# FFN up projections by seven block products instead of eight, with a separate down phase and a new grid for the operand pools

## The chip, the cores and the metric

The kernel runs on one core of a Trainium2 chip. The metric is the device time of one execution in microseconds (us), as the median of several runs; less is better. Engines: TensorE (PE; PEld is its weight load), VectorE (DVE), ScalarE (ACT), GpSimd (POOL), and SyncE (SP), which issues most DMA transfers.

## What is computed

Two layers of a decoder trunk on 1024 tokens of width 1024, all in float32. Layer 0 mixes with latent attention (MLA), layer 1 with a gated spatial unit (gMLP). What the change touches is the FFN that follows each mixer; after it a gated embedding (PLE) is added:

```python
for i in range(2):
    h = h + mixer_i(rms_norm(h, norm_mix[i]))          # mla_mixer / gmlp_mixer, ends in @ w_out
    hn = rms_norm(h, norm_ffn[i])                      # 1024 x 1024
    h = h + square(relu(hn @ ffn_w_up[i])) @ ffn_w_down[i]    # 1024 -> 4096 -> 1024
    hn = rms_norm(h, norm_ple[i])
    h = h + sigmoid(hn @ ple_w_gate[i]) * (p[i] @ ple_w_proj[i])
```

## The kernel before

The residual stream `h` stands in SBUF with features on the partitions: eight tiles `h0` to `h7` of 128 features x 1024 tokens. A float32 product is made of three TensorE products of operands split into a high and a low half (`split`: ScalarE casts the high half, VectorE subtracts it for the low one): high x high, high x low, low x high. A matmul has a 128x128 block of weights as its stationary operand and 512 tokens as its moving one.

`load_block` fetches 128x4 rows x 256 columns of weights (512 KB) by DMA into `raw` (pool `pr`, 3 buffers) and splits it into `wh` and `wl` (pool `pw`). `gemm` issues the matmuls of one block of 128 output rows into PSUM. `Norm.add` prepares the next phase's input as soon as a tile of `h` is final: `add_split` scales it by the gain and splits it into pool `phn`, `add_square` adds its square to `acc`. The factor 1/rms is applied only after the product: `sums` adds up `acc` over the partitions with four matmuls, `roots` takes the inverse root on ScalarE and VectorE.

`ffn` goes through the 4096 hidden features in eight slices of 512. For each slice it makes the up products (4 row blocks x 2 halves of the tokens x 8 blocks of depth x 3 = 192 matmuls), applies ReLU, the norm factor and the square, splits the result into `ah` and `al` (pool `pa`), and at once makes the slice's part of the down product (`down_slice`, another 192 matmuls) and adds it to `h`; the last slice goes through `down_sweeps`, which also prepares the next norm. Ahead of the FFN stands the mixer's output projection, a `down_slice` too: `wo1` in layer 0, `go3` in layer 1, in four blocks of 256 output rows. Behind each two tiles of `h` that it finishes, `nxt.add` prepares the FFN's input.

Nothing but the order of the program and the buffers of the pools sets the order on an engine: each engine takes its instructions in the order in which a scheduler has put them, and a pool hands its buffers out in program order.

SBUF addresses: the operand pools `pa`, `pw`, `pr`, `ph`, `pt` begin at 800 modulo 2048 bytes, `pb` at 832 behind its small `lead` tile, `phn` at 864.

Of the kernel before, what the change touches and what calls it, by code (L numbers as in the profile page):

```python
# [16 lines left out]
P = 128  # L17
T = 1024
# [14 lines left out]
QB, PB = 2, 2  # L33
LNEXP = "natural_log_exp_and_others"
# [5 lines left out]
def trunk(ctx: ExitStack, tc: tile.TileContext, I, out):  # L40
# [6 lines left out]
    pw = ctx.enter_context(tc.tile_pool(name="pw", bufs=6))  # L47
# [32 lines left out]
    G.memset(pb.tile([P, 8], F32, tag="lead", name="lead"), 0.0)  # L80
# [89 lines left out]
    class Norm:  # L170
# [72 lines left out]
        def tokens(self, c, pp=None):  # L243

            if self.r is None:
                self.r = pb.tile([P, NB], F32, tag="rtok", name=f"{self.name}_r")
# [4 lines left out]
            V.tensor_copy(self.r[:, c * 4:c * 4 + 4], pp.rearrange("p (b q) -> p b q", q=P)[:, :, 0])  # L251


    halves = {}

    def ffn(i, h, nrm, nxt, late):
        up, down = I["ffn_w_up"][i], I["ffn_w_down"][i]
        for s in range(FF // 512):
            ah = pa.tile([P, 4, T], F32R, tag="a", name=f"f{i}_ah{s}")
            al = pa.tile([P, 4, T], F32R, tag="a", name=f"f{i}_al{s}")  # L260
            for g in range(2):
                f0 = s * 512 + g * 256
                bl = [load_block(up, k0, f0) for k0 in (0, 4)]
                for f in range(2):
                    units = gemm(bl, nrm.hn, f, f"f{i}u{s}{g}{f}")
                    if nrm.rb is None:
                        for c in range(2):
                            nrm.sums(c, pso(f"f{i}st{c}"))
                        nrm.roots(0, 1)
                    rb = nrm.rb  # L270
                    t = tmp(f"f{i}t{s}{g}{f}")
                    k = 2 * g + f
                    for u, c in units:
                        V.scalar_tensor_tensor(t[:, c], u, 0.0, rb[:, c], op0=ALU.max, op1=ALU.mult)  # L274
                        S.activation(t[:, c], t[:, c], AF.Square)  # L275
                        S.copy(ah[:, k, c], t[:, c])
                        V.tensor_tensor(al[:, k, c], t[:, c], f32(ah[:, k, c]), op=ALU.subtract)
            rhs = chunked(ah, al, 4)
            if s == 1:
                halves[i] = p_split(i)  # L280
            if s < FF // 512 - 1:
                down_slice(down, 4 * s, rhs, h, f"f{i}d{s}", None)
            else:
                down_sweeps(down, 4 * s, rhs, h, f"f{i}d{s}", nxt, late)

    def down_slice(w, k0, rhs, h, name, nxt, seq=False):
        for q in range(4):
            bl = [load_block(w, k0, q * 256)]
            for f in range(2):
                j = 2 * q + f  # L290
# [96 lines left out]
    def gmlp(h, nrm, nxt):  # L387
# [85 lines left out]
        for gp in range(4):  # L473
# [58 lines left out]
            down_slice(w_out, 4 * gp, chunked(yh, yl, 4), h, f"go{gp}", nxt if gp == 3 else None, seq=True)  # L532
# [584 lines left out]
    n1 = Norm("n1", gain(1, 0))  # L1117
# [50 lines left out]
```

## Time and profile before

| | |
|---|---|
| median of 3 runs | 2728.8 us (2728.18 to 2729.13) |
| profiled execution, its own time | 2726.77 us |
| its span | 2725.0 us |
| granted TensorE clock, mean | 0.999 |
| TensorE busy, matmuls | 2691.1 us, 13600 |
| VectorE, ScalarE, GpSimd busy | 1228.5, 903.2, 317.0 us |
| DMA | 163.54 MB, mean 60 GB/s |

The profile shows one execution. Busy times are sums over all stages; what a stage waits for is read in the chain of waits, which follows the work that ended last back through the span, and in the timeline. Line numbers L.. are those of the kernel.

### The profile page before, as it was taken

Reading aid. Unit: us, or ns where it says so; the run is one execution under the profiler, and the core shown is the slowest. Engines: PE = TensorE matmul, PEld = TensorE weight load, DVE = VectorE, ACT = ScalarE, POOL = GpSimd, SP = SyncE. Lnnn points to the kernel's source line nnn. Section 1 sums busy time; section 2 is a strip of 40 time slices with the busy share of each in tenths; the row PEclk is TensorE's granted clock in tenths of the full one; section 3 lists DMA queues with packets and bytes.
Section 4 is the critical chain, followed back from the end, with each engine's and each line's share of the span. In section 5 each row is a group of like instructions: output and inputs, shape, how many; then the busy total and the mean of one; then the engine's idle time right before and its main releaser. Section 6 shows DMA issues by size and latency. Waiting matters only on the chain.

```text
span 2725.0 us, 33466 instructions
## 1 busy us (share of the span) xinstructions
PE 2691.1 (99%) x13600; PEld 2281.4 (84%) x13600; DVE 1228.5 (45%) x1964; ACT 903.2 (33%) x1815; POOL 317.0 (12%) x460
## 2 busy tenths in 40 slices
PE   8999999999999999999999999999999999999999
PEld 7999888888888888888888788888888888888899
DVE  6777774533333333375522534436433333333652
ACT  4677772411221122164422312214221112211541
POOL 4444330000000000001211332030000000000000
PEclk9999999999999999999999999999999999999999
DMA  5100012111111111132332312211111111111221
GB/s 166 53 18 5 24 55 70 47 47 62 54 47 47 47 52 49 35 99 76 103 103 95 95 41 84 86 40 62 47 62 47 47 55 47 51 50 39 66 94 36
DMA packets 151209, 163.54 MB, mean 60 GB/s; under 512 B 6496, under 2 KB 133024, under 8 KB 151056
## 3 DMA queue, kind: packets, MB, share of 16 engines
q1 hardware_dynamic: 146240, 146.31, 17.3%
q0 software_dynamic: 4816, 15.10, 1.8%
q8 instruction: 107, 1.75, 0.3%
q14 instruction: 46, 0.38, 0.0%
HBM read 144.61 MB, written 16.78 MB: 59 GB/s over the span
## 4 chain that ended last, share of the span: by engine, by line
PE 87%; DVE 4%; ACT 4%; issue 1%; DMA 1%; POOL 1%; POOLq 0%; ACTq 0%; DVEq 0%
PE f1u L64 13%; PE f0u L64 13%; PE f0d L64 13%; PE f1d L64 12%; PE up L64 6%; PE vp L64 6%; PE go L64 6%; PE e L64 4%; PE wo L64 3%; PE pg L64 3%; PE s L64 2%; PE pq L64 1%; PE av L64 1%; PE pk L64 1%; PE sv L64 1%
## 5 line engine op out<-in xcount | busy, mean ns | idle before, releaser
L110 ACT CAST wh<-raw 128x1024 fp32r<-128x1024 f32 x160 | 168.3, 1052 | 777.7 <-PE f1d L64 258.8
L111 DVE TENSOR_TENSOR wl<-raw,wh 128x1024 fp32r<-128x1024 f32 x160 | 195.1, 1219 | 65.1 <-ACT wh L110 56.7
L292 DVE TENSOR_TENSOR h<-f1d,h 128x512 f32<-128x512 f32 (+1 forms) x84 | 70.4, 866 | 192.0 <-PE f1d L64 192.0
L292 DVE TENSOR_TENSOR h<-f0d,h 128x512 f32<-128x512 f32 (+1 forms) x84 | 70.4, 866 | 192.0 <-PE f0d L64 192.0
L64 PE MATMUL f1d<-f_ah,wh 128*128 128x512 f32 x448 | 138.2, 390 | 0.0
L64 PE MATMUL f0d<-f_ah,wh 128*128 128x512 f32 x448 | 138.2, 390 | 0.0
L64 PE MATMUL f1d<-f_al,wh 128*128 128x512 f32 x448 | 138.1, 390 | 0.0
L64 PE MATMUL f0d<-f_al,wh 128*128 128x512 f32 x448 | 138.1, 390 | 0.0
L64 PE MATMUL f1d<-f_ah,wl 128*128 128x512 f32 x448 | 138.0, 389 | 0.0
L64 PE MATMUL f0d<-f_ah,wl 128*128 128x512 f32 x448 | 137.9, 389 | 0.0
L349 POOL TENSOR_TENSOR h<-sig,h 128x512 f32<-128x512 f32 x16 | 22.0, 1392 | 887.7 <-DVE sig L348 868.3
L274 DVE SCALAR_TENSOR_TENSOR f0t<-f0u,n_rb 128x512 f32<-128x512 f32 (+1 forms) x48 | 40.2, 866 | 172.1 <-PE f0u L64 172.0
L274 DVE SCALAR_TENSOR_TENSOR f1t<-f1u,n_rb 128x512 f32<-128x512 f32 (+1 forms) x48 | 40.2, 866 | 172.1 <-PE f1u L64 172.0
L64 PEld LDWEIGHTS f1d<-f_ah,wl 128*128 128x128 f32 x448 | 84.1, 188 | 17.7
L64 PEld LDWEIGHTS f0d<-f_ah,wl 128*128 128x128 f32 x448 | 84.1, 188 | 17.6
L64 PEld LDWEIGHTS f0d<-f_al,wh 128*128 128x128 f32 x448 | 84.1, 188 | 17.6
L64 PEld LDWEIGHTS f1d<-f_al,wh 128*128 128x128 f32 x448 | 84.1, 188 | 17.6
L64 PEld LDWEIGHTS f0d<-f_ah,wh 128*128 128x128 f32 x448 | 84.0, 188 | 17.4
L64 PEld LDWEIGHTS f1d<-f_ah,wh 128*128 128x128 f32 x448 | 84.0, 188 | 17.4
L275 ACT ACTIVATE f0t<-f0t 128x512 f32<-128x512 f32 (+1 forms) x48 | 36.8, 772 | 156.9 <-DVE f0t L274 156.9
L275 ACT ACTIVATE f1t<-f1t 128x512 f32<-128x512 f32 (+1 forms) x48 | 36.8, 772 | 156.9 <-DVE f1t L274 156.9
L64 PE MATMUL go<-yh,wh 128*128 128x512 f32 x256 | 84.2, 393 | 1.8 <-ACT yh L110 1.8
(2174 smaller groups left out, 7216.9 us busy)
## 6 DMA issues: line engine op xcount, KB each, us to landing
raw<-in_ffn_w_up_dram SPq DMA_DIRECT2D x64, 512.0 KB, 3.7
raw<-in_ffn_w_down_dram SPq DMA_DIRECT2D x56, 512.0 KB, 3.4
raw<-in_ffn_w_down_dram SPq DMA_DIRECT2D x32, 256.0 KB, 2.8
raw<-in_ple_w_gate_dram SPq DMA_DIRECT2D x16, 512.0 KB, 3.7
vr<-vpark SPq DMA_DIRECT2D x16, 512.0 KB, 3.7
raw<-in_gmlp_w_out_dram SPq DMA_DIRECT2D x16, 512.0 KB, 3.5
vpark<-vg POOLq DMA_DIRECT2D x24, 256.0 KB, 2.3
x<-in_x_dram SPq DMA_DIRECT2D x8, 512.0 KB, 3.9
```

The source lines that it names most:

```text
L64: PE.matmul(o, l, r, start=start, stop=stop)
L110: S.copy(hi, src)
L111: V.tensor_tensor(lo, src, f32(hi), op=ALU.subtract)
L274: V.scalar_tensor_tensor(t[:, c], u, 0.0, rb[:, c], op0=ALU.max, op1=ALU.mult)
L275: S.activation(t[:, c], t[:, c], AF.Square)
L292: V.tensor_tensor(h[j][:, c], u, h[j][:, c], op=ALU.add)
L349: G.tensor_tensor(h[j][:, cs], sg, h[j][:, cs], op=ALU.add)
```

## The change

**Seven products.** `wino_up` takes the up product as 2x2 blocks: two row blocks of 128 outputs, the depth in four pairs `q` of 128-blocks, the tokens in two halves. Seven products of sums and differences of blocks (`PRODUCTS`) stand in place of eight, 84 matmuls for a pair of row blocks in place of 96. `NormX.add_pair` makes the token side for a pair of tiles of `h`: B21, B11, T1, T2, B22, and T3, T4 (in `rest` those of T3 and T4 that `early` does not name). `wino_weights` makes the weight side: A11, A12, A22 from `raw`, S1 to S4 from sums on GpSimd, seven tiles for each pair, split as before. Three products open a PSUM bank (`OPENS`), the others add onto it after VectorE or ScalarE has read the partial sum that stands there.

**Two phases.** The hidden activations go to DRAM (`apark`, 32 rows of 512 KB a layer) and come back in `slice_in` for eight down slices that follow the whole up phase. `h` goes to DRAM too (`hpark`) and comes back with the first slice.

**Pools.** `pw` has 8 buffers, there is a new pool `pe`; `lead` moves to `const` with 304 words, `rtok` too, and all operand pools begin at 0 modulo 2048 bytes. The scratch of software DMA is 4096 bytes.

TensorE has 13216 instructions in place of 13600.

```diff
-    pw = ctx.enter_context(tc.tile_pool(name="pw", bufs=6))
+    pw = ctx.enter_context(tc.tile_pool(name="pw", bufs=8))
...
-    G.memset(pb.tile([P, 8], F32, tag="lead", name="lead"), 0.0)
+    G.memset(const.tile([P, LEAD], F32, name="lead"), 0.0)
...
+        def add_pair(self, q, h):
+            n = f"{self.name}_{q}"
+            u = [tmp(f"{n}u{e}", [P, 2, 512]) for e in range(2)]
+            for e in range(2):
+                S.activation(u[e].rearrange("p c t -> p (c t)"), h[2 * q + e], AF.Copy, scale=self.g[2 * q + e])
+            a = tmp(f"{n}a", [P, 2, 512])
+            b = pw.tile([P, 2, 512], F32, tag="w", name=f"{n}b")
+            G.tensor_tensor(a[:, 0], u[0][:, 1], u[0][:, 0], op=ALU.subtract)
+            V.tensor_tensor(b[:, 0], u[1][:, 1], u[0][:, 1], op=ALU.subtract)
+            self.put("B21", q, u[1][:, 0])
+            self.put("B11", q, u[0][:, 0])
+            V.tensor_tensor(a[:, 1], u[1][:, 1], a[:, 0], op=ALU.subtract)
+            self.put("T1", q, a[:, 0])
+            V.tensor_tensor(b[:, 1], u[1][:, 0], a[:, 1], op=ALU.subtract)
+            self.put("T2", q, a[:, 1])
+            self.put("B22", q, u[1][:, 1])
+            for c, src in (("T3", b[:, 0]), ("T4", b[:, 1])):
+                if c in self.early:
+                    self.put(c, q, src)
+                else:
+                    self.kept[c, q] = src
+            for e in range(2):
+                k = 2 * q + e
+                if self.acc is None:
+                    self.acc = pb.tile([P, T], F32, tag="acc", name=f"{self.name}_acc")
+                    S.activation(self.acc, h[k], AF.Square)
+                else:
+                    sq = tmp(f"{n}sq{e}")
+                    S.activation(sq, h[k], AF.Square)
+                    G.tensor_tensor(self.acc, sq, self.acc, op=ALU.add)
+                nc.sync.dma_start(self.hpark[k], h[k])
+        def rest(self):
+            for c in ("T3", "T4"):
+                for q in range(4):
+                    if (c, q) in self.kept:
+                        self.put(c, q, self.kept.pop((c, q)))
...
+    def wino_weights(w, f0):
+        name = f"wx{cnt[0]}_"
+        cnt[0] += 1
+        raw = []
+        for j in range(2):
+            r = pr.tile([P, 4, 256], F32, tag="raw", name=f"{name}r{j}")
+            nc.sync.dma_start(r, w[j * 512:(j + 1) * 512, f0:f0 + 256].rearrange("(k p) f -> p k f", p=P))
+            raw.append(r.rearrange("p (q e) (g f) -> p q e g f", e=2, g=2))
+        def quad(j, e, g):
+            return raw[j][:, :, e, g, :]
+        sa, sb = (ph.tile([P, 2, 4, 128], F32, tag="h", name=f"{name}s{x}") for x in "ab")
+        for j in range(2):
+            js = slice(2 * j, 2 * j + 2)
+            G.tensor_tensor(sa[:, 0, js], quad(j, 0, 1), quad(j, 1, 1), op=ALU.add)
+        for j in range(2):
+            js = slice(2 * j, 2 * j + 2)
+            G.tensor_tensor(sa[:, 1, js], sa[:, 0, js], quad(j, 0, 0), op=ALU.subtract)
+        for j in range(2):
+            js = slice(2 * j, 2 * j + 2)
+            G.tensor_tensor(sb[:, 0, js], quad(j, 1, 0), sa[:, 1, js], op=ALU.subtract)
+        for j in range(2):
+            js = slice(2 * j, 2 * j + 2)
+            G.tensor_tensor(sb[:, 1, js], quad(j, 0, 0), quad(j, 0, 1), op=ALU.subtract)
+        for what in ("A12", "A11", "S1", "S2", "S4", "S3", "A22"):
+            wslot[0] = (wslot[0] + 1) % 12
+            pool, tag = (ph, "h") if wslot[0] % 12 < 4 else (pw, "w")
+            t = pool.tile([P, 2, 4, 128], F32R, tag=tag, name=f"{name}{what}")
+            if what[0] == "A":
+                e, g = int(what[2]) - 1, int(what[1]) - 1
+                for j in range(2):
+                    js = slice(2 * j, 2 * j + 2)
+                    split(t[:, 0, js], t[:, 1, js], quad(j, e, g))
+            else:
+                src = {"S1": sa[:, 0], "S2": sa[:, 1], "S4": sb[:, 0], "S3": sb[:, 1]}[what]
+                split(t[:, 0], t[:, 1], src)
+            yield t
+    PRODUCTS = [("B21", "y"), ("B11", "x"), ("T1", "z"), ("T2", "x"), ("B22", "z"), ("T3", "x"), ("T4", "x")]
...
+    OPENS = {0, 1, 2}
...
+            def run(i, qs=range(4)):
+                while len(wt) <= i:
+                    wt.append(next(gen))
+                c, b = PRODUCTS[i]
+                product_x(bank[b], wt[i], nrm.x[c], i in OPENS, qs)
+            def prepare():
+                if nxt is not None:
+                    ready.append(next(nxt))
+            if n == 0:
+                for qs in (range(3), range(3, 4)):
+                    for i in range(3):
+                        run(i, qs)
+                scale(u)
+            else:
+                run(0)
+            S.copy(e0[:, 0], bank["y"])
+            if late is not None:
+                late()
+            prepare()
+            if n > 0:
+                run(1)
+            V.tensor_tensor(row[0][:, 0], bank["x"], e0[:, 0], op=ALU.add)
+            prepare()
+            if n > 0:
+                run(2)
+            S.copy(e0[:, 1], bank["z"])
+            prepare()
+            run(3)
+            S.copy(e1, bank["x"])
+            prepare()
+            run(4)
+            V.tensor_tensor(row[0][:, 1], bank["z"], e1, op=ALU.add)
+            rb = nrm.rb
+            r0 = row[0].rearrange("p c t -> p (c t)")
+            V.scalar_tensor_tensor(r0, r0, 0.0, rb, op0=ALU.max, op1=ALU.mult)
+            S.activation(r0, r0, AF.Square)
+            out(2 * n, r0)
+            prepare()
+            run(5)
+            V.tensor_tensor(row[1][:, 1], bank["x"], e0[:, 1], op=ALU.add)
+            V.scalar_tensor_tensor(row[1][:, 1], row[1][:, 1], 0.0, rb[:, CS[1]], op0=ALU.max, op1=ALU.mult)
+            S.activation(row[1][:, 1], row[1][:, 1], AF.Square)
+            prepare()
+            side(n)
+            prepare()
+            def last():
+                run(6)
+                V.scalar_tensor_tensor(row[1][:, 0], bank["x"], 0.0, rb[:, CS[0]], op0=ALU.max, op1=ALU.mult)
+                S.activation(row[1][:, 0], row[1][:, 0], AF.Square)
+                out(2 * n + 1, row[1].rearrange("p c t -> p (c t)"))
+            return nxt, ready, last
...
-    def ffn(i, h, nrm, nxt, late):
+    def ffn(i, nrm, nxt, late, first, h=None):
         up, down = I["ffn_w_up"][i], I["ffn_w_down"][i]
...
+        apark = pd.tile([FF // P, P, T], F32, name=f"f{i}_apark")
+        def out(k, row):
+            nc.sync.dma_start(apark[k], row)
+        def slice_in(s):
+            rhs = []
+            if s % 2:
+                ah, al = (pa.tile([P, 4, T], F32R, tag="a", name=f"f{i}_a{x}{s}") for x in "hl")
+            for k in range(4):
+                raw = pr.tile([P, T], F32, tag="raw", name=f"f{i}ar{s}{k}")
+                nc.sync.dma_start(raw, apark[4 * s + k])
+                if s % 2:
+                    split(ah[:, k], al[:, k], raw)
+                    rhs.append([(ah[:, k, CS[c]], al[:, k, CS[c]]) for c in range(2)])
+                else:
+                    row = []
+                    for c in range(2):
+                        hi, lo = (phn.tile([P, 512], F32R, tag="hn", name=f"f{i}a{s}{k}{c}{x}") for x in "hl")
+                        split(hi, lo, raw[:, CS[c]])
+                        row.append((hi, lo))
+                    rhs.append(row)
+                yield rhs
+        gen = [slice_in(0)]
+        rhs = []
+        def side(n):
+            if n == FF // 256 - 1:
+                for _ in range(4):
+                    rhs.append(next(gen[0]))
+        wino_up(up, FF, nrm, first, f"f{i}u", out, side)
+        cur = rhs[-1]
+        h = [] if h is None else h
+        for s in range(NS):
             if s == 1:
                 halves[i] = p_split(i)
```

How the change moves instructions is seen at three places in the order of the engines. The names: `n1` is the norm ahead of layer 0's FFN, its digits the pair `q` or the tile and the half; `wh5` to `wh9` the weight blocks of the output projection, `wx6`, `wx9` the weights of the first two pairs, `f0u8g` the PSUM banks x and z of pair 8.

ScalarE in layer 0's output projection, before, from the cast of its first block:

```order
L110 CAST wh5_5789<-raw5_5787 128x1024
L110 CAST wh6_5874<-raw6_5872 128x1024
L110 CAST wh7_5962<-raw7_5960 128x1024
L188 ACTIVATE n1_00h_5819<-h0_5418,gT_94 128x512
L198 ACTIVATE n1_acc_5823<-h0_5418 128x512
L188 ACTIVATE n1_01h_5825<-h0_5418,gT_94 128x512
L198 ACTIVATE n1_acc_5823<-h0_5418 128x512
L110 CAST wh8_6050<-raw8_6048 128x1024
L188 ACTIVATE n1_10h_5858<-h1_5420,gT_94 128x512
```

And now, behind the same cast (which stands some rows earlier):

```order
L279 ACTIVATE n1_0u0_5851<-h0_5418,gT_94 128x1024
L300 ACTIVATE n1_acc_5878<-h0_5418 128x1024
L279 ACTIVATE n1_0u1_5852<-h1_5420,gT_94 128x1024
L111 CAST n1T1_0_5868<-n1_0a_5855 128x512
L111 CAST n1B210h_5859<-n1_0u1_5852 128x512
L303 ACTIVATE n1_0sq1_5881<-h1_5420 128x1024
L111 CAST n1B110h_5863<-n1_0u0_5851 128x512
L111 CAST n1T2_5872<-n1_0a_5855 128x512
L111 CAST n1B22_5875<-n1_0u1_5852 128x512
L111 CAST wh6_5887<-raw6_5885 128x1024
```

Three more blocks were cast ahead of the norm's work or between its first rows; now the second block `wh6` stands behind the whole preparation of the first two tiles of `h`, and `wh8` and `wh9` stand in the same way behind that of the next two pairs. The difference tiles `n1_0b` take buffers of the same pool `pw`, and stand ahead of them in the program.

TensorE in a steady pair (layer 0, the end of pair 7); there is no such place before, where no product adds onto a bank that has been read:

```order
L389 MATMUL f0u7g_7264<-n1T33l_6208,wx15_S3_7256 128x512
L389 MATMUL f0u7g_7264<-n1T33h_6207,wx15_S3_7256 128x512
L389 MATMUL f0u8g_7409<-n1B112h_6073,wx16_A11_7330 128x512
L389 MATMUL f0u8g_7409<-n1B112l_6074,wx16_A11_7330 128x512
L389 MATMUL f0u8g_7409<-n1B112h_6073,wx16_A11_7330 128x512
L389 MATMUL f0u8g_7409<-n1B113h_6172,wx16_A11_7330 128x512
L389 MATMUL f0u7g_7264<-n1T40h_6211,wx15_A22_7259 128x512
L389 MATMUL f0u7g_7264<-n1T40l_6212,wx15_A22_7259 128x512
```

VectorE at the same place of pair 8, from the row behind the product S4:

```order
L446 TENSOR_TENSOR f0u8a0_7413<-f0u8g_7409,f0u8u2_7412 128x512
L449 SCALAR_TENSOR_TENSOR f0u8a0_7413<-f0u8a0_7413,n1_rb_6290 128x1024
L454 TENSOR_TENSOR f0u8a1_7414<-f0u8g_7409,f0u8e_7411 128x512
L112 TENSOR_TENSOR wx19_A22_7839<-wx19_r0_7733,wx19_A22_7839 128x256
L455 SCALAR_TENSOR_TENSOR f0u8a1_7414<-f0u8a1_7414,n1_rb_6290 128x512
L463 SCALAR_TENSOR_TENSOR f0u8a1_7414<-f0u8g_7409,n1_rb_6290 128x512
```

Between the last matmul of S3 and the first of A22, both on bank x, stand four matmuls of the next pair; VectorE's L454 reads the bank in between. The splits of weights for later pairs stand between such rows.

TensorE at the row sums of layer 0, before:

```order
L64 MATMUL f0u000_6150<-n1_70l_6123,wh10_6146 128x512
L64 MATMUL f0u000_6150<-n1_71l_6130,wh10_6146 128x512
L64 MATMUL f0u000_6150<-n1_70h_6122,wl10_6147 128x512
L64 MATMUL f0u000_6150<-n1_71h_6129,wl10_6147 128x512
L64 MATMUL f0st0_6199<-n10_shl_6200,onesr_86 128x512 x2
L64 MATMUL f0st1_6205<-n11_shl_6206,onesr_86 128x512 x2
L64 MATMUL f0u001_0_6232<-n1_00h_5819,wh9_6140 128x512
```

and now, with ScalarE's rows of the same time below:

```order
L389 MATMUL f0u0g_6236<-n1T1_1_6078,wx6_S1_6094 128x512 x3
L65 MATMUL f0u0st0_6278<-n10_shl_6279,onesr_86 128x512
L65 MATMUL f0u0st1_6284<-n11_shl_6285,onesr_86 128x512
L65 MATMUL f0u0st0_6278<-n10_shl_6279,onesr_86 128x512
L65 MATMUL f0u0st1_6284<-n11_shl_6285,onesr_86 128x512
L389 MATMUL f0u1y_6395<-n1B210h_5859,wx9_A12_6321 128x512
L389 MATMUL f0u1y_6395<-n1B210l_5860,wx9_A12_6321 128x512
L389 MATMUL f0u1y_6395<-n1B210h_5859,wx9_A12_6321 128x512
L389 MATMUL f0u0g_6236<-n1T2_5872,wx6_S2_6129 128x512 x12
```

```order
L236 ACTIVATE n10_vr_6293<-n1_rb_6290 128x512
L231 ACTIVATE n1_rb_6290<-f0u0st1_6284,epst_87 128x512
L234 ACTIVATE n11_vr_6300<-f0u0st1_6284,epst_87 128x512
L235 ACTIVATE n1_rb_6290<-n1_rb_6290 128x512
L430 COPY f0u0e_6238<-f0u0y_6237 128x512
L236 ACTIVATE n11_vr_6300<-n1_rb_6290 128x512
L111 CAST wx9_A12_6321<-wx9_r0_6307 128x256
L111 CAST wx9_A12_6321<-wx9_r1_6309 128x256
```

Behind the sums stood matmuls on a block that had been split long before; now stand three that need A12 of the second pair, `wx9_A12`, which ScalarE splits behind the roots.

## Rows read from the trace of the kernel before

**Rows 1.** The page, parts 1 and 4: busy time by engine; the chain by engine.
```profile
PE 2691.1 (99%) x13600; PEld 2281.4 (84%) x13600; DVE 1228.5 (45%) x1964; ACT 903.2 (33%) x1815; POOL 317.0 (12%) x460
...
PE 87%; DVE 4%; ACT 4%; issue 1%; DMA 1%; POOL 1%; POOLq 0%; ACTq 0%; DVEq 0%
```

**Rows 2.** The chain of waits, 420 to 700 us: start, length, what ran.
```profile
423.43 76.64 PE wo L64 x336
500.07 10.99 PE f0u L64 x48
511.06 0.94 PE f0st L64 x4
512.00 32.98 PE f0u L64 x144
544.97 43.57 PE f0d L64 x192
588.54 43.97 PE f0u L64 x192
```

**Rows 3.** The chain elsewhere: gate, gMLP up, last projection, MLA keys and values.
```profile
1203.73 43.96 PE pg L64 x192
...
1815.49 5.60 PE up L64 x24
...
2628.88 3.46 PE e L64 x30
...
143.55 1.42 PE pk L64 x12
```

**Rows 4.** Busy time by stretch: window, length, engines (instructions), granted clock, DMA, GB/s.
```profile
0.00:10.00 10.00, 3.84 (x17) 3.36 (x18) 3.27 (x12) 4.28 (x6) 6.99 (x50) 1.00 0.76 176
423.00:500.00 77.00, 77.00 (x341) 63.47 (x341) 43.67 (x59) 27.11 (x43) 0.00 (x0) 1.00 0.24 76
545.00:589.00 44.00, 44.00 (x195) 36.38 (x195) 16.30 (x20) 6.95 (x9) 0.00 (x0) 1.00 0.16 48
```

**Rows 5.** ScalarE: groups by form (count, busy, mean ns), and a timeline row.
```profile
L110 ACT CAST wh<-raw 128x1024 fp32r<-128x1024 f32 x160 | 168.3, 1052 | 777.7 <-PE f1d L64 258.8 <-PE f0d L64 258.8 <-PE f0u L64 78.8
...
L846 ACT CAST v<-pk 128x256 fp32r<-128x256 f32 x32 | 11.9, 373 | 16.1 <-DVE tq L845 15.5
...
L226 ACT ACT_TABLE_LOAD x7 | 9.0, 1283 | 0.1
...
7.76 1.06 ACT L691 CAST xh<-xp 128x512 fp32r<-128x512 f32 x2
```

**Rows 6.** VectorE: groups by form, and a timeline row (start, length).
```profile
L111 DVE TENSOR_TENSOR wl<-raw,wh 128x1024 fp32r<-128x1024 f32 x160 | 195.1, 1219 | 65.1 <-ACT wh L110 56.7 <-issue 4.3 <-PE pg L64 4.1
...
L292 DVE TENSOR_TENSOR h<-f0d,h 128x512 f32<-128x512 f32 x56 | 36.1, 686 | 111.7 <-PE f0d L64 111.7
...
L292 DVE TENSOR_TENSOR h<-f0d,h 128x1024 f32<-128x1024 f32 x28 | 34.3, 1225 | 80.3 <-PE f0d L64 80.3
...
L111 DVE TENSOR_TENSOR vhl<-vr,vhl 128x512 fp32r<-128x512 f32 x32 | 25.1, 784 | 19.3 <-ACT vhl L110 19.1
...
L847 DVE TENSOR_TENSOR v<-pk,v 128x256 fp32r<-128x256 f32 x32 | 13.5, 423 | 8.9 <-ACT v L846 8.9
...
434.16 1.29 DVE L1110 TENSOR_TENSOR h<-wo,h 128x512 f32<-128x512 f32 x2 [3.73 <-PE wo L64]
```

**Rows 7.** GpSimd: groups by form.
```profile
L349 POOL TENSOR_TENSOR h<-sig,h 128x512 f32<-128x512 f32 x16 | 22.0, 1392 | 887.7 <-DVE sig L348 868.3 <-ACT sig L339 14.0 <-issue 5.4
...
L706 POOL TENSOR_TENSOR xs<-xh,xl 128x1024 f32<-128x1024 f32 x8 | 19.4, 2420 | 42.0 <-ACT xs L705 19.1 <-ACT rl2r L1094 6.0 <-ACT rl5r L1094 5.7
```

**Rows 8.** DMA: bandwidth in 40 slices of the span; one issue, last its us to landing.
```profile
GB/s 166 53 18 5 24 55 70 47 47 62 54 47 47 47 52 49 35 99 76 103 103 95 95 41 84 86 40 62 47 62 47 47 55 47 51 50 39 66 94 36
...
h<-park SPq DMA_DIRECT2D x8, 512.0 KB, 4.4
```

**Rows 9.** ScalarE's timeline, 430 to 447 us, in the output projection.
```profile
444.81 1.05 ACT L110 CAST wh<-raw 128x1024 fp32r<-128x1024 f32 x1 [9.82 <-PE wo L64]
```

More of the change, by code (lines that the diff above doesn't have):

```diff
@@ L245, in tokens @@
             if self.r is None:
[L246 removed]
+                self.r = const.tile([P, NB], F32, tag="rtok", name=f"{self.name}_r")
             if pp is None:
@@ new lines, in trunk, with product_x, wino_up, scale @@
+    PRODUCTS = [("B21", "y"), ("B11", "x"), ("T1", "z"), ("T2", "x"), ("B22", "z"), ("T3", "x"), ("T4", "x")]
+    OPENS = {0, 1, 2}
+    def product_x(o, t, xs, first, qs=range(4)):
+        for q in qs:
+            hi, lo = xs[q]
+            wh, wl = t[:, 0, q], t[:, 1, q]
+            st = first and q == 0
+            for l, r, x, y in ((wh, hi, st, False), (wh, lo, False, False), (wl, hi, False, q == 3)):
+                PE.matmul(o, l, r, start=x, stop=y, skip_group_check=not first)
+    def wino_up(w, F, nrm, first, nm, out, side):
+        nfp = F // 256
+        def scale(u):
+            if nrm.rb is None:
+                for c in range(2):
+                    nrm.sums(c, pso(f"{u}st{c}"))
+                nrm.roots(0, 1)
+            return nrm.rb
+        def pair(n, gen, wt, late):
+            u = f"{nm}{n}"
+            nxt = wino_weights(w, (n + 1) * 256) if n + 1 < nfp else None
+            ready = []
+            g = psg(f"{u}g")
+            bank = {"x": g[:, CS[0]], "z": g[:, CS[1]], "y": pso(f"{u}y")}
+            e0 = tmp(f"{u}e", [P, 2, 512])
+            e1 = pe.tile([P, 512], F32, tag="e", name=f"{u}u2")
+            row = [tmp(f"{u}a{x}", [P, 2, 512]) for x in range(2)]
+            def run(i, qs=range(4)):
[49 more added lines that the diff above has]
+            return nxt, ready, last
+        gen, ready = first
+        late = None
+        for n in range(nfp):
+            gen, ready, late = pair(n, gen, ready, late)
+        late()
@@ L254, in trunk @@
     halves = {}
-    def ffn(i, h, nrm, nxt, late):
+    NS = FF // 512
+    def ffn(i, nrm, nxt, late, first, h=None):
         up, down = I["ffn_w_up"][i], I["ffn_w_down"][i]
[L258 to L278, printed above, removed]
@@ L287, in down_slice @@
+        return h
+    def down_slice(w, k0, rhs, h, name, nxt, seq=False, before=None, after=None):
         for q in range(4):
@@ L1116, in trunk @@
     phn = ctx.enter_context(tc.tile_pool(name="phn", bufs=32))
-    n1 = Norm("n1", gain(1, 0))
+    pe = ctx.enter_context(tc.tile_pool(name="pe", bufs=1))
+    n1 = NormX("n1", gain(1, 0), place0, ("T2", "B22"))
     rhs1 = []
```

89 lines of the change are left out of this document (73 added, 16 removed).

## Prediction

> **What bounds the kernel now.** I read the page first: TensorE is busy 99% of the span and holds 87% of the chain [rows 1], so time is won only by taking matmuls away, and lost wherever TensorE is made to stand. The chain of waits then gives the speed of each kind. An up slice is 192 matmuls in 43.97 us, a down slice 192 in 43.57 us, directly behind each other, and the output projection ahead of them 336 in 76.64 us without a piece of another engine between [rows 2]. Start to start that is 229.0, 226.9 and 228.1 ns. In gMLP a 512-column matmul takes 5.60/24 = 233.3 ns; 256-column ones take 3.46/30 = 115.3 ns in the last projection and 1.42/12 = 118.3 ns in the MLA keys and values [rows 3]. Busy time by stretch shows the slack beside this: in the output projection VectorE works 43.7 and ScalarE 27.1 of 77 us, in a down slice 16.3 and 7.0 of 44, GpSimd nothing [rows 4].
>
> The profiled execution took 2726.8 us, the median of the runs is 2728.8; I sum against the first and add 2.0 at the end.
>
> **Fewer matmuls.** Before, 16 up slices of 43.97 us: 703.5 us. Now each layer has 16 pairs of row blocks of 7 x 12 = 84 matmuls: 2688. Their operands are now all at the same offset in 2048 bytes, as moving and stationary operand of the down slices already are, so I take that stage's 226.9 ns: 609.9 us, **-93.6 us**. At 229.0 ns it would be -88.0.
>
> **The grid elsewhere.** The 1344 512-column matmuls of gMLP's two halves (768 and 576) would go from 233.3 to 226.9 ns, -8.6 us; 384 of the gate from 229.0 (43.96 us for 192, [rows 3]) to 226.9, -0.8. The 1344 of 256 columns (960 of the last projection, 384 of gMLP) stand at 115.3; if they go to the 118.3 of the keys and values, +4.0. Together **-5.4 us**; bounds -9.4 (256 columns unchanged) and +4.0 (512 unchanged).
>
> **A steady pair.** TensorE 84 x 226.9 ns = 19.1 us. VectorE: six half weight tiles at 0.423, four at 0.686, five epilogue rows at 0.686 and one at 1.225 [rows 6]: 9.9 us. ScalarE: six at 0.373, four casts, three copies and two squares at 0.53 (half of the pair in 1.06), a square at 1.06 [rows 5]: 8.1 us. GpSimd: eight sums of 256 columns, at half of 1.392 us each [rows 7]: 5.6 us. DMA: two weight tiles in and two rows out, 2.1 MB in 19.1 us, 110 GB/s, where slices of the span carry 103 and 166 [rows 8]. All have room. One wait is tight: in the second order excerpt A22 adds onto the bank that VectorE's L454 must first have read, and only four matmuls (0.91 us) stand between. L454 takes 0.69 and no split is ahead of it here: nothing lost. Where one is (1.37 together) it costs 0.5. I take a quarter of 32 pairs: **+4 us**; bounds 0 and 45 (two splits at 0.784, the row beside GpSimd, ahead of a read of the same length: 2.35 - 0.91 = 1.4 us in each pair).
>
> **The start of an up phase** is where I see the change pay. The three later weight blocks of the projection were cast before: ScalarE did a block in 1.05 us and then waited 9.8 us for TensorE [rows 9]. Now each stands on ScalarE behind the preparation of a pair of rows (first excerpt), which begins only when TensorE has finished that pair. From the last matmul of the first pair in layer 0: two additions to h, 1.29; u1, 1.05; two differences on VectorE, 1.29 (the same form as the additions); T1 0.53, B21 0.53, square 1.05, B11, T2, B22 1.59, wh6 1.05; wl6 on VectorE 1.22 [rows 5, 6]. That is 9.6 us, less the four matmuls that need wh6 alone, 0.9: TensorE stands 8.7 us. Row by row in the same way: wh8 10.5 (it also stands behind a second square and A12 of the first pair's weights), wh9 10.3; in layer 1 8.1, 10.9 and 8.6. Sum **+57 us**. Before, this time was nil.
>
> Then the first pair itself. In layer 0 TensorE has 36 matmuls (8.2 us) and then wants the row sums. The last two squares end at 7.3 and 8.4 us after the projection, GpSimd adds each to the sum in 2.42 us [rows 7], one behind the other, 12.2; two casts and the low halves, 14.5. TensorE stands 5.6. Next it wants A12 of the second pair, which ScalarE splits behind the table load (1.28), four casts and nine rows of roots and copies: 23 us, against 14.7 for the end of the sums: 8.2 more. In layer 1 the same two waits come to 5 and 6, because more is split ahead. **+25 us**. With three stalls before them in each layer that makes ten in all. Bounds of both sums: 40 us, if ScalarE's casts run ahead of what I add up by a third and half the second wait goes; 100, if every hop between engines adds 0.2 us.
>
> **Up to down.** The activations are read back as 512 KB rows, one of this size landing in up to 4.4 us [rows 8], four matmul groups ahead of their use; the write of a slice lies phases earlier. Splitting them costs VectorE and ScalarE what the old splits did, on stages with half their time free [rows 4]. I take **+4 us** for the two first slices, with h loaded again; bounds 0 and 10. The smaller DMA scratch and the lead tile: nothing, at bounds of 2 either way.
>
> **Sum:** -93.6 - 5.4 + 4 + 57 + 25 + 4 = -9.0: 2717.8, and against the median **2720 us**.
>
> **The rivals.**
> 1. *The starts cost half.* Against it: engines take their rows in order, and the excerpt's order is fixed. For it: my chain adds whole durations where some overlap. With 45 instead of 82 it gives 2683. Chance 0.18.
> 2. *The grid does more than level the stages.* No stage of before is on it, only on equal offsets. A 512-column matmul at 226.9 has 13.6 ns above 512 columns at the 2.4 GHz of the granted clock of 1.00; the last projection has 8.6 above 256. If the former fell to that, the change's some 8,700 matmuls of 512 columns (counted in its order) gain 5.0 ns each, 43 us: 2677. Chance 0.09. The Trainium skill, "TensorE: Matmul & The Clock Gate" (Wait — 56ns, not 53.3ns?), gives 215.7 ns for 512 columns; by it the gain would be an estimated 97 us, and no row here comes near it.
> 3. *The stalls cost more than their length* (slower): TensorE stands 5 to 11 us ten times, and the clock may fall to 1.2 GHz there. The profile speaks against it as far as it goes: in the first 10 us TensorE worked 3.84 and the granted clock was 1.00 [rows 4], but no row shows ten idle us. The 48 matmuls of the block behind a stall, 10.9 us, would at half speed cost at most 10.9 us more; from 0.9 us a stall it eats the gain; at 3.5 it gives 2755. Chance 0.20. The same page of the Trainium skill (What you observe; What's actually happening) says that an idle array drops to 1.2 GHz and comes back after sustained work; by that this rival holds.
> 4. *Pairs starve* (slower): VectorE late at L454 in every pair, 1.4 us as bounded above, from 0.4 us deciding: 2761. VectorE's splits do take longer beside GpSimd's work, 0.784 against 0.686 [rows 6]. Chance 0.13. The Trainium skill, "SBUF — State Buffer" (the section on who interferes with whom), has VectorE with two SBUF inputs wait out a GpSimd instruction altogether; the row's 0.1 us speaks for a milder form.
>
> **How the numbers follow.** The forecast has 0.40 and its own range is 2700 to 2740. A measurement can tell about 0.2%, 5.5 us: faster is below 2723. The forecast gives 0.23 faster, 0.08 same, 0.09 slower; rivals 1 and 2 give 0.27 faster; 3 and 4 give 0.02 faster, 0.03 same and 0.28 slower. Faster **0.52**, same **0.11**, slower **0.37**. The range reaches to rivals 1, 3 and 4 but leaves out most of what the grid could give beyond 43 us and the largest clock cost: 2658 to 2772.
>
> **What would show it.** Right: up pieces of 84 matmuls in 19.1 us; TensorE waiting on ScalarE's wh or VectorE's wl three times in each projection ahead of an up phase, 8 to 11 us; then on the row sums and on A12. Granted clock 1.00 throughout. Wrong: no such waits, or short ones (rival 1); down slices under 43 us (2); a granted clock well below 1 in the 20 us around the starts (3); a wait on L454 in most pairs (4).

## The result, and the profile after

| | before | after |
|---|---|---|
| median | 2728.89 us (4 runs) | 2806.28 us (2800.76 to 2807.97, 4 runs) |
| ratio, 95% interval | | 1.0282 (1.0270 to 1.0295) |
| span of the profiled execution | 2725.0 us | 2806.2 us |
| granted clock, mean | 0.999 | 0.975 |

The change is slower by 2.8%. It was forecast to be slightly faster, and the time lies above the stated range. The page of after, busy times and the granted clock in 40 slices (tenths):

```profile
PE 2654.2 (95%) x13216; PEld 2224.5 (79%) x13216; DVE 1461.8 (52%) x2336; ACT 1050.4 (37%) x2191; POOL 598.4 (21%) x738
...
PEclk9999999789999999999999999997899999999999
```

There are 384 matmuls fewer than in [rows 1] and 37 us less of TensorE's work, but 118 us more in which it does nothing, and two places with a clock below 9 tenths: the output projections ahead of the up phases, with the first pairs behind them. What TensorE waited for (engine, line, what ended the wait: us in total, times, longest):

```profile
PE wo L65 <- ACT wh L111: 24.1, 3, 8.4
PE go L65 <- ACT wh L111: 22.6, 3, 9.7
PE wo L65 <- DVE wl L112: 9.5, 3, 3.6
PE go L65 <- DVE wl L112: 9.3, 3, 3.9
...
PE f0u1y L389 <- ACT wx_A L111: 5.7, 1, 5.7
PE f0u0st L65 <- ACT n_shl L209: 5.0, 2, 4.8
PE f1u1y L389 <- ACT wx_A L111: 4.8, 1, 4.8
...
PE f0u11g L389 <- ACT f0u11u L443: 2.2, 1, 2.2
```

The three stands in each projection are there, as forecast, each made of a wait for `wh` and one for `wl`: 33.6 us in wo (forecast 29.5), 31.9 in go (27.6). The first of them on TensorE's timeline (start, length, what; in brackets the idle time before):

```profile
471.47 0.61 PE L65 MATMUL wo<-oh,wl 128*128 128x512 f32 x2
479.43 1.22 PE L65 MATMUL wo<-oh,wh 128*128 128x512 f32 x2 [7.34 <-ACT wh L111]
480.45 1.05 PE L65 MATMUL wo<-ol,wh 128*128 128x512 f32 x2
485.12 1.22 PE L65 MATMUL wo<-oh,wl 128*128 128x512 f32 x2 [3.62 <-DVE wl L112]
486.14 1.05 PE L65 MATMUL wo<-oh,wh 128*128 128x512 f32 x2
...
489.41 0.62 PE L65 MATMUL wo<-ol,wh 128*128 128x512 f32 x2
```

Two waits stand here: 7.3 us for `wh`, then after four matmuls 3.6 us for `wl`. Behind each, pairs of matmuls follow at 0.85 to 1.0 us, where 0.45 is full speed: the array runs at 1.2 GHz, until 489.4 us; the granted clock is on record as half from 475.6, inside the first wait. ScalarE at the same time, then VectorE and GpSimd:

```profile
473.22 1.15 ACT L279 ACTIVATE n_0u<-h,gT 128x1024 f32<-128x1024 f32 x1 [3.18 <-DVE h L545]
...
477.81 0.61 ACT L111 CAST n1B<-n_0u 128x512 fp32r<-128x512 f32 x1
478.33 1.04 ACT L111 CAST wh<-raw 128x1024 fp32r<-128x1024 f32 x1
```

```profile
476.56 0.68 DVE L112 TENSOR_TENSOR n1T<-n_0a,n1T 128x512 fp32r<-128x512 f32 x1
477.16 2.84 DVE L288 TENSOR_TENSOR n_0b<-n_0u,n_0a 128x512 f32<-128x512 f32 x1
479.93 1.21 DVE L112 TENSOR_TENSOR n1B110l<-n_0u,n1B110h 128x512 fp32r<-128x512 f32 x1
...
483.33 1.74 DVE L112 TENSOR_TENSOR wl<-raw,wh 128x1024 fp32r<-128x1024 f32 x1
```

```profile
476.95 2.50 POOL L304 TENSOR_TENSOR n_acc<-n_0sq,n_acc 128x1024 f32<-128x1024 f32 x1 [2.21 <-ACT n_0sq L303]
479.42 2.31 POOL L362 TENSOR_TENSOR wx_sb<-wx_r,wx_sa 128x256 f32<-128x256 f32 x2
```

ScalarE is as forecast: the cast stands behind the preparation of the pair. VectorE is not. Its L288 takes 2.84 us, a form that takes 0.69 otherwise [rows 6], and ends 0.55 us behind GpSimd's addition of squares, about its own length; the three rows behind it take 1.21 each, about as long as one of GpSimd's sums (2.31 for two). Over the whole kernel the splits of weights show the same: of the 192 of 256 columns, 129 met no instruction of GpSimd and took 0.407 to 0.427 us, and 63 met one and took 0.82 in the mean, 2.58 at most. The additions to `h` in go, which read one of their two inputs from PSUM, take 0.686 with or without GpSimd at work.

A steady stretch holds waits too. Busy time by window (columns as in [rows 4]), the first projection and then 13 pairs of layer 0, which begin at 595.1 and 863.2 us, 20.6 us each where 84 matmuls need 19.1:

```profile
470.00:550.00 80.00, 46.35 (x160) 35.12 (x159) 42.60 (x44) 24.66 (x36) 29.81 (x21) 0.72 0.16 59
595.00:863.00 268.00, 259.52 (x1094) 201.00 (x1093) 136.03 (x208) 106.07 (x207) 85.62 (x100) 0.99 0.31 108
```

One of these waits, TensorE and ScalarE in pair 6:

```profile
702.67 2.98 PE L389 MATMUL f0u6g<-n1T,wx_S 128*128 128x512 f32 x12
...
706.40 0.39 PE L389 MATMUL f0u7g<-n1B110h,wx_A 128*128 128x512 f32 x1
708.32 3.01 PE L389 MATMUL f0u6g<-n1B,wx_S 128*128 128x512 f32 x12 [1.53 <-ACT f0u6u L443]
```

```profile
703.97 0.41 ACT L111 CAST wx_A<-wx_r 128x256 fp32r<-128x256 f32 x1 [1.11 <-DMA wx_r<-in_ffn_w_up_dram]
706.35 0.62 ACT L111 CAST wx_S<-wx_sa 128x512 fp32r<-128x512 f32 x1 [1.98 <-POOL wx_sa L359]
707.16 0.62 ACT L111 CAST wx_S<-wx_sb 128x512 fp32r<-128x512 f32 x1 [0.19 <-POOL wx_sb L362]
707.68 0.58 ACT L443 COPY f0u6u<-f0u6g 128x512 f32<-128x512 f32 x1
```

The product S4 (`f0u6g<-n1B`) writes bank z, and waits for L443, which reads bank x. In ScalarE's order L443 stands behind three casts for later pairs, which waited for a transfer and for GpSimd's sums.

**Where the 81 us are.** I add the distances from start to start, each given to the later matmul and so to the tile that this one writes:

| us | before | after | forecast of the change |
|---|---|---|---|
| wo | 87.4 | 131.1 | +29.5 |
| go | 175.3 | 219.4 | +27.6 |
| f0u, f1u with the row sums | 705.3 | 692.4 | -93.6 + 25 + 4 |
| f0d, f1d with their row sums | 698.0 | 697.6 | +4 at the start |
| up, vp of gMLP; gate; last projection | 355.0; 88.9; 117.0 | 348.9; 87.1; 119.4 | -5.4 in all |

The grid came out as forecast (-5.5 in the last row); the 4 us at the start of the down phases did not come. Some 12 us more lie in the rest, 5 of them ahead of wo and 6 in gMLP's `yp`, where waits for VectorE's `u` grew from 2.0 to 7.8 us. The 84 MB more of DMA traffic are not what slows the kernel: the fastest one below moves as much (247.5 MB).

### The profile page after: what moved, and what is told of

Its sections match the earlier page's. It is cut to its first block, busy times and chain, and to the rows that moved or that the text cites. A ratio compares the mean times of both kernels' runs of the same rounds, so it can differ in the third digit from the quotient of the medians.

```text
span 2806.2 us, 34481 instructions
## 1 busy us (share of the span) xinstructions
PE 2654.2 (95%) x13216; PEld 2224.5 (79%) x13216; DVE 1461.8 (52%) x2336; ACT 1050.4 (37%) x2191; POOL 598.4 (21%) x738
## 5 line engine op out<-in xcount | busy, mean ns | idle before, releaser
L111 ACT CAST wh<-raw 128x1024 fp32r<-128x1024 f32 x96 | 101.0, 1052 | 321.7 <-PE f0d L65 115.9
L112 DVE TENSOR_TENSOR wx_A<-wx_r,wx_A 128x256 fp32r<-128x256 f32 x192 | 99.2, 552 | 116.9 <-ACT wx_A L111 116.2
L112 DVE TENSOR_TENSOR wl<-raw,wh 128x1024 fp32r<-128x1024 f32 x96 | 122.9, 1280 | 48.8 <-ACT wh L111 42.4
L545 DVE TENSOR_TENSOR f0h<-f0d,f0h 128x512 f32<-128x512 f32 (+1 forms) x84 | 70.3, 865 | 145.8 <-PE f0d L65 145.7
L545 DVE TENSOR_TENSOR f1h<-f1d,f1h 128x512 f32<-128x512 f32 (+1 forms) x84 | 70.3, 865 | 139.4 <-PE f1d L65 139.4
L65 PE MATMUL go<-yh,wl 128*128 128x512 f32 x256 | 87.6, 409 | 9.3 <-DVE wl L112 9.3
L111 ACT CAST wx_A<-wx_r 128x256 fp32r<-128x256 f32 x192 | 70.9, 404 | 58.5 <-DMA wx_r<-in_ffn_w_up_dram 37.7
L65 PE MATMUL go<-yl,wh 128*128 128x512 f32 x256 | 88.5, 413 | 0.0
L65 PE MATMUL s<-kT,q 128*128 128x512 f32 (+5 forms) x288 | 73.1, 357 | 2.3 <-DVE q L112 1.8
L65 PE MATMUL av<-pt,v 128*128 128x256 f32 (+1 forms) x480 | 64.0, 283 | 5.0 <-DVE sm L1238 2.4
```

Of the source, the lines that this page charges most:

```text
L65: PE.matmul(o, l, r, start=start, stop=stop)
L111: S.copy(hi, src)
L112: V.tensor_tensor(lo, src, f32(hi), op=ALU.subtract)
```

## The experiments

All but the grid alone are edits of the changed kernel or of each other, and all are timed beside runs of the kernel before on their chip (2727 to 2729 us).

**The projection's next block ahead of the rows' preparation.**

```diff
                 if nxt is not None and j % 2:
+                    if q < 3:
+                        ahead = [load_block(w, k0, (q + 1) * 256)]
                     nxt.add_pair(j // 2, h)
```

> The changed kernel with one edit: in the output projections ahead of an up phase (wo1, go3) the next weight block is loaded and split before the pair of rows is prepared, not behind it. Theory A (the three waits in each projection, 65 us of TensorE standing on wh and wl, and the half clock that follows them, come only from the place of these casts in ScalarE's order): the projection wo goes from 131 back to about 88 us, go from 232 to about 183, no wait of TensorE on wh over 1 us there, granted clock 1.00 in them; total near 2715 us. Rival B (the preparation of the rows bounds the projection whatever the order, since ScalarE, VectorE and GpSimd need 9 to 10 us for each pair and a block of matmuls lasts 10.9): waits move to the additions or to the splits, total above 2770. Rival C (waits go, but move to the start of the up phase, where the first pair then stands longer): projections fall by 90 us, up phases grow by 20 or more, total 2735 to 2760.

Measured: 2745.95 us, ratio 1.0071 (1.0056 to 1.0087), 60 us less. wo takes 95.3 us and go 184.8 (the expectation's 232 for go gives each distance to the earlier matmul; counted so, go falls from 231.8 to 196.9), and the waits for `wh` are gone but for one of 1.8 us in go. Theory A holds for two thirds of it: most of the waits that stay there are for `wl` of the last blocks, and the up phases grow by 11 us (theory C in part). Some of TensorE's waits:

```profile
PE wo L65 <- DVE wl L112: 6.1, 2, 4.1
PE f1u0st L65 <- ACT n_shl L209: 6.1, 1, 6.1
...
PE go L65 <- DVE wl L112: 5.5, 2, 3.2
```

**Bank z a tile of its own.**

```diff
-            bank = {"x": g[:, CS[0]], "z": g[:, CS[1]], "y": pso(f"{u}y")}
+            bank = {"x": g[:, CS[0]], "z": pso(f"{u}z"), "y": pso(f"{u}y")}
```

> The changed kernel with one edit: in a pair, bank z is a tile of its own, no longer the second half of the tile that holds bank x. Theory A (each of the five later products of a pair waits for the reader of the product before it, although that reader reads the other bank, because the two banks are one tile; only four matmuls stand between): the waits on S1, S2 and S4 go, S3 and A22 keep theirs; the 28 us over 60 ns in the pairs 2 to 15 of both layers fall to below 12, up matmuls' mean spacing without large gaps goes from 230.5 to about 228 ns, total 2771 to 2785 us. Rival B (pairs stand because weight transfers and splits are late, so the wait moves to the weight tiles): less than 8 us gained, total above 2798, and TensorE's waits name wx tiles.

Measured: 2767.24 us, 1.0142 (1.0128 to 1.0156), 39 us less, more than theory A said. The 13 pairs from 603.6 to 854.9 us take 19.3 each, and TensorE is busy 248.6 of 251 us:

```profile
604.00:855.00 251.00, 248.59 (x1092) 204.37 (x1091) 134.34 (x201) 104.70 (x201) 82.89 (x96) 1.00 0.33 118
```

In the pairs 2 to 15 of both layers the distances ahead of the matmuls of S4 exceeded 227 ns by 18.4 us in the changed kernel and exceed it by 0.1 here; those of S1 and S2 go from 6.1 to nothing, and those of S3 and A22 stay (11.2 and 11.4), all as theory A has it. The first two pairs gain another 8 us, which it had not counted. So the change had made each later product of a pair wait for the reader of the product before, whichever bank it read.

**Matmuls into the standing time.**

```diff
             bl = [load_block(w, k0, q * 256)]
+            if nxt is not None and q > 0:
+                d = pso(f"{name}warm{q}")
+                for _ in range(36):
+                    mm(d, onesr, rhs[0][0][0], True, True)
```

> The changed kernel plus 36 matmuls (8.2 us at full speed) onto a PSUM tile that nothing reads, in TensorE's order ahead of each of the second to fourth blocks of wo1 and go3, where TensorE stands 10 to 12 us; the result is not touched and the stall itself stays. Theory A (113 matmuls of the projections run at 1.2 GHz because TensorE stood before them, at 227 ns more each, 26 us, and some of the first pairs too): no stretch at half clock in the two projections, total 2770 to 2782 us, though 216 matmuls more are issued. Rival B (the half clock is only a record, the time is set by ScalarE's chain): total within 6 us of the changed kernel's 2806, or longer.

Measured: 2800.44 us, 1.0262 (1.0248 to 1.0276), 5.8 us less with 216 matmuls more. The granted clock of wo's stretch goes from 0.72 to 0.91:

```profile
470.00:550.00 80.00, 69.21 (x272) 54.55 (x271) 42.81 (x44) 25.49 (x37) 30.01 (x21) 0.91 0.17 62
```

The three waits for `wl` behind the fill still let it fall. Matmuls at 400 to 500 ns in the two projections cost some 17 us above 227 ns each in the changed kernel and 9 here; theory A's 113 matmuls at 227 ns more are 86 at 200. Its total fails, and the number of rival B holds by a hair (5.8 of at most 6 us). wo and its fill together take 130.3 us, hardly less than wo's 131.1 without; go and its fill take 212.6, against 219.4. The run does not price the clock, since the fill can also be too long: in the first stall `wh` was there at 479.9 us and the next product began at 480.7. What the slow matmuls cost above 227 ns is 22 us over the whole kernel (17, and 5 in the up phases). That is an upper bound, as some of them run while `wl` is still missing, and far from most of the loss.

**The grid alone**, on the kernel before.

```diff
-    G.memset(pb.tile([P, 8], F32, tag="lead", name="lead"), 0.0)
+    G.memset(const.tile([P, LEAD], F32, name="lead"), 0.0)
...
-                self.r = pb.tile([P, NB], F32, tag="rtok", name=f"{self.name}_r")
+                self.r = const.tile([P, NB], F32, tag="rtok", name=f"{self.name}_r")
...
-    nc = _bacc.Bacc("TRN2", target_bir_lowering=False, num_devices=1)
+    nc = _bacc.Bacc("TRN2", target_bir_lowering=False, num_devices=1, dynamic_dma_scratch_size=4096)
```

> The kernel before with only the pools' grid of the change: lead of 304 words and rtok in const, smaller DMA scratch, all operand pools at 0 modulo 2048. Theory A (only the offset between moving and stationary operand counts): up matmuls 229.0 to 227 ns, -6 us for 3072; gMLP's 1344 of 512 columns 233.3 to 227, -8.5; gate -0.8; 1344 of 256 columns 115.5 to 120, +6; total 2719 us, 0.3 to 0.4% faster. Rival B (standing on the grid itself matters): down slices fall below 43 us, total under 2700. Rival C (no effect beyond noise): 2726 to 2731.

Measured: 2716.85 us, 0.9957 (0.9944 to 0.9969). Theory A to within 2 us. In the chain, an up slice now takes what a down slice takes (43.97 before, [rows 2]), and a down slice what it took:

```profile
545.19 43.52 PE f0d L65 x192
588.71 43.53 PE f0u L65 x192
```

So the offset between the two operands counts, not the grid as such: the down slices, whose operands had the same offset before, got no faster. The smaller DMA scratch and the place of `rtok` went in with it and were not timed apart.

**Row sums and roots behind the fifth product** of the first pair.

```diff
-                scale(u)
...
-            rb = nrm.rb
+            rb = scale(u)
             r0 = row[0].rearrange("p c t -> p (c t)")
```

> The changed kernel with one edit: in the first pair of an up phase the row sums and roots stand behind the fifth product, just ahead of the first use of the factor, no longer behind the third. Theory A (TensorE stands on the row sums, 11 us in both layers, and on A12 of the second pair, 10.5 us, only because both come that early and the roots stand ahead of that split on ScalarE): most of the 21 us go, 24 more matmuls (5.4 us) cover the sums; total 2787 to 2794 us. Rival B (the preparation as a whole is late, the wait moves to the operands T2, B22 or to the banks): less than 6 us gained, total above 2800.

Measured: 2797.08 us, 1.0255 (1.0241 to 1.0269), 9 us less, between the theories. The wait on A12 of the second pair goes; the sums are still waited for (14.5 us).

**Three edits together** (block ahead, own banks, sums later).

> The three edits together: the projection's next block ahead of the rows' preparation, bank z a tile of its own, row sums behind the fifth product. Theory A (the three waits are separate and their costs add: 60 us of the first and 39 of the second as measured, 12 to 18 of the third): 2687 to 2697 us, faster than the kernel before by 1.2 to 1.5% and than the grid alone (2717) too. Rival B (they overlap, a wait taken away shows the next): 2705 to 2725.

Measured: 2706.26 us, 0.9921 (0.9907 to 0.9935). Rival B's range: 100 of the 108 us add up.

**And the first pair's weights later** in the projection.

```diff
-            if j >= 3:
+            for _ in range({5: 3, 6: 1, 7: 1}.get(j, 0)):
                 ready.append(next(gen))
```

> The three edits, and the first pair's weights are split later in the projection (three tiles behind the third pair of rows, none ahead of the fourth weight block). Theory A (the 4.1 and 3.2 us that TensorE still waits for wl of the last blocks come from A12 and A11, which stand ahead of that block on ScalarE and VectorE): these waits fall below 1.5 us each and the half clock behind them goes, 5 to 12 us under the three edits. Rival B (the late splits are missed at the start of the up phase): TensorE waits for A12, A11 or S1 of the first pair instead, the same time as the three edits or more.

Measured: 2706.38 us, 0.9920 (0.9907 to 0.9934): rival B in time. wo falls from 95.8 to 88.4 us and f0u grows from 328.8 to 337.4; there TensorE waits 5.0 us for the high half of B21 on ScalarE, not for the weights that rival B names.

**T3 and T4 left over split behind the first copies** (the call of `rest` moved into the first pair, ahead of its fourth product), on the three and on the four edits.

> The three edits, and the splits of T3 and T4 that are left over stand behind the first pair's two copies from PSUM, not ahead of the pair. Theory A (in the three edits TensorE stands 4.8 and 6.0 us on the copy of bank z and 3.3 us on B21, because up to eight casts of T3 and T4 stand ahead on ScalarE): these waits fall below 2 us each, total 2692 to 2699 us. Rival B (T3 and T4 are then late, TensorE waits for them or for A12 of the second pair): 2702 us or more.

Measured: 2700.95 us, 0.9897 (0.9882 to 0.9912), 5 us less; between the theories.

> The same with the four edits. Theory A as above, and no waits on wl in wo: 2690 to 2698 us. Rival B (the work ahead of the up phase is a sum that ScalarE and VectorE have to do at some place before TensorE can run, and each shift only moves the wait): 2702 us or more, with wo and go shorter and the up phases longer by as much.

Measured: 2702.31 us, 0.9901 (0.9885 to 0.9918): rival B by a hair, the shift of the weights gains nothing here either. Moving work about had come to its end; VectorE's long rows were the next suspect.

**Nothing of the change on GpSimd but one difference a pair of rows.**

```diff
-                    G.tensor_tensor(self.acc, sq, self.acc, op=ALU.add)
+                    V.tensor_tensor(self.acc, sq, self.acc, op=ALU.add)
...
-            G.tensor_tensor(sa[:, 0, js], quad(j, 0, 1), quad(j, 1, 1), op=ALU.add)
+            V.tensor_tensor(sa[:, 0, js], quad(j, 0, 1), quad(j, 1, 1), op=ALU.add)
...
```

> The changed kernel with the sums of weight tiles and the additions of squares on VectorE, none on GpSimd. Theory A (an instruction of VectorE with two inputs in SBUF stands while GpSimd works: in the first stall one of 0.69 us took 2.84 beside an addition of squares of 2.50, and wl came 3.6 us late): the waits for wl in wo and go, 18.8 us in all, fall below 8, splits in the pairs go from 552 and 820 ns back to about 425 and 690, total 2780 to 2794 us. Rival B (what counts is the amount of work; VectorE gets 3.4 us of sums a pair and 1.2 us an addition more, and its queue grows): 2800 us or more.

Measured: 2746.94 us, 1.0076 (1.0059 to 1.0092): 59 us less, far more than theory A said. The first stall on VectorE's timeline, in this run:

```profile
475.65 0.68 DVE L288 TENSOR_TENSOR n_0b<-n_0u,n_0a 128x512 f32<-128x512 f32 x1
...
479.19 1.22 DVE L112 TENSOR_TENSOR wl<-raw,wh 128x1024 fp32r<-128x1024 f32 x1
```

The splits of all pairs in the changed kernel:

```profile
L112 DVE TENSOR_TENSOR wx_A<-wx_r,wx_A 128x256 fp32r<-128x256 f32 x192 | 99.2, 552 | 116.9 <-ACT wx_A L111 116.2
L112 DVE TENSOR_TENSOR wx_S<-wx_sa,wx_S 128x512 fp32r<-128x512 f32 x64 | 56.1, 880 | 35.0 <-ACT wx_S L111 34.0
```

And in this run:

```profile
L112 DVE TENSOR_TENSOR wx_A<-wx_r,wx_A 128x256 fp32r<-128x256 f32 x192 | 74.6, 418 | 59.1 <-ACT wx_A L111 58.9
L112 DVE TENSOR_TENSOR wx_S<-wx_sa,wx_S 128x512 fp32r<-128x512 f32 x64 | 43.5, 687 | 16.2 <-ACT wx_S L111 16.1
```

L288 takes 0.68 us in place of 2.84, `wl` 1.22 in place of 1.74, and ends 2.7 us behind `wh`, not 5.7. The waits for `wl` fall from 18.8 to 0.7 us. VectorE's busy time is 1485.0 us against 1461.8, although it now does the 256 sums and 14 additions that GpSimd did, some 125 us at its own rates (256 at 0.42, 14 at 1.22): about 100 us of its busy time had been standing.

The run takes two things away at once: GpSimd's instructions beside VectorE's, and their slower rate (a sum of 256 columns took 0.72 us or more on GpSimd, 0.42 on VectorE). wo and go lose 35 us, the first two pairs of both layers 11, the other pairs 15. In the projections the waits for `wl`, 18 of those 35 us, are VectorE's standing. In the pairs the two are not told apart: ScalarE's casts had also waited 24.4 us for GpSimd's sums.

**The same on the best kernel so far**, squares alone, then all.

> The kernel with three edits and T3, T4 later (2701 us), with the additions of squares on VectorE; the sums of weight tiles stay on GpSimd. Theory A (the same): the wl waits of 12.2 us fall below 6 and the row sums come earlier, since an addition takes 1.23 in place of 2.42 us; total 2686 to 2696 us. Rival B: 2699 us or more.

Measured: 2676.83 us, 0.9816 (0.9801 to 0.9830), 24 us less.

> The same with the sums of weight tiles on VectorE too. Theory A: splits are never held up, pairs lose less, wl waits below 4 us; total 2678 to 2692 us, under the squares alone. Rival B (in the pairs the sums on VectorE make its queue late for the reads of the banks): above the squares alone, by more than 4 us.

Measured: 2653.36 us, 0.9726 (0.9711 to 0.9740), another 23 us. Theory A in both, with more than it said. This kernel beats the one before by 2.7%, and the grid alone by 63 us. Its page:

```profile
PE 2599.2 (98%) x13216; PEld 2216.6 (84%) x13216; DVE 1483.6 (56%) x2606; ACT 1049.7 (40%) x2191; POOL 332.1 (13%) x468
...
PEclk9999999999999999999999999999999999999999
```

Its up phases take 629.2 us, 76 less than before with the row sums, about its whole gain; wo takes 87.5 and go 174.0, as before the change.

## Why the prediction was wrong

The forecast was -9.0 us, and +81.2 came (2726.8 to 2808.0 in the profiled executions): a miss of 90 us. The stalls at the starts were forecast in the right places. Three steps failed: a steady pair was priced at +4 us, because each PSUM bank was taken to wait for its own reader; GpSimd's work beside VectorE was priced at 0.1 us a row; and the clock at nothing. The sum's terms against what the trace shows:

- **Matmuls and grid, -93.6 and -5.4: right.** Start to start is 227 ns in up, down and gMLP, and 120 in the last projection (118.3 taken). Rival 2 fell: no down slice got shorter.
- **The three stalls of each projection, +57: right in place and cause, low in size.** 65.5 us of waits, +8. The walk had `wl` 1.22 us behind `wh`; in the first stall it came 5.7 behind (479.4 to 485.1), since VectorE's queue was late. The block-ahead run confirms the cause of the waits for `wh`, the run without GpSimd that of the waits for `wl`.
- **The first pairs, +25: low.** The long distances in the first two pairs of both layers exceed 227 ns by 43.9 us in all, some 5 of them the clock's: +14. The waits named were there (5.0 and 5.7 us in layer 0; forecast 5.6 and 8.2), others came with them.
- **A steady pair, +4: wrong, +33.** The forecast's 609.9 us and 1.9 for the row sums, taken from 692.4 with those 43.9, leave 36.7. I named one tight wait and gave the other four products room, counting banks. The program waits by tiles, and x and z were one tile, so all five products had only four or five matmuls of cover; what then made the readers late, in the pair shown, were casts that stood ahead of them and waited for a transfer and for sums. Rival 4 had the effect (VectorE at L454) and a bound of 45 us, but the wrong row: in the pairs 2 to 15 the distances ahead of S4, which waits for L443, exceed 227 ns by 18.4 us, ahead of S3 by 6.6, ahead of A22, which waits for L454, by 4.6, ahead of S1 and S2 by 6.1. With bank z a tile of its own some 11 of these 36 us are left.
- **Up to down, +4: -0.4.** The first slices were covered, although 4.4 us in [rows 8] is the median landing and not the longest.
- **The clock, 0 in the sum: up to 22 us.** Rival 3 was real, at some 2 us a stall and not 3.5, and the row held against it was misread (below the list).
- **GpSimd beside VectorE, counted as 0.1 us a row: 59 us, as much as the order of the casts (60).** It lies inside the terms above that came out high, and GpSimd's slower rate may be part of it. I had read 0.784 against 0.686 [rows 6] as a mild contention. Of these 32 rows 25 met no instruction of GpSimd and took 0.685 us; the other seven took 0.81 to 1.64. The mean hides how long one that meets it stands. The Trainium skill, "SBUF — State Buffer" (Who interferes with whom), says that a VectorE instruction with two SBUF inputs contends with a GpSimd instruction that reads SBUF, and calls the shared port an exclusive lock; the 2.84 us beside a 2.50 us addition agree.

**The misread row.** [rows 4] gives a granted clock of 1.00 for the first 10 us of the kernel before, with 3.84 us of work. But the trace has no record of the clock ahead of 16.55 us, and the view counts a stretch without a record as 1.00. The matmuls show what the array did. A product of 384 columns and one of 320, ahead of 16.55 us and behind it:

```profile
11.82 0.79 PE L64 MATMUL lat<-wdh,xl 128*128 128x384 f32 x2
...
16.79 0.48 PE L64 MATMUL lat<-wdh,xl 128*128 128x384 f32 x2
```

The 384 columns take 320 ns from start to start in the first, which is 1.2 GHz, and 177 in the second. So this kernel too began at half clock. The Trainium skill, "TensorE: Matmul & The Clock Gate" (What's actually happening), says that the default state is throttled and that activity releases it; the start of this trace and the stands of the other agree.

The terms come to 73 of the 90 us (8, 14, 33 and 22, less 4). The rest, 5 us in the projections and 12 in other stages, was not pursued. That the causes add is shown roughly: block, banks and GpSimd alone gave 60, 39 and 59, with the 9 and 5 us of the two moves at the start 172; all five together gave 153.

## What to carry to other kernels

Before giving side work to GpSimd, look at what VectorE runs beside it: here an instruction with two inputs in SBUF stood until GpSimd's had ended, and a mean over rows that mostly ran alone did not show it. When one engine's idle time is to be filled with the preparation of the next phase, put what the present phase still needs ahead of it in the program, and give each PSUM bank that is read and written in turn a tile of its own. A stall of TensorE costs its length and then some: here up to 2 us more each at half clock. A granted clock of 1.00 is worth only as much as its record: the spacing of the matmuls tells what the array did.

## What had not been expected of the hardware

- The clock falls within a stand of 7.3 us and also stays low through one of 3.6: in the first stall it was half from 475.6 us for 13.7 us, of which TensorE worked some 6.
- The same weight cast takes 0.40 us on ScalarE with or without GpSimd at work (404 and 405 ns for 256 columns); of these two engines only VectorE is held up.
- At 512 columns an equal offset of both operands is the faster (227 against 229 and 233 ns), at 256 the slower (120 against 115 to 116), in the grid run against the kernel before. Why this is so stays open.
